# A hybrid decoder layer on one core: the exponential's bias on VectorE, and one more key block of every score tile turned by DMA

## The chip, the cores and the metric

The kernel runs on one core of a Trainium2 chip. The metric is the device time of one execution in microseconds (us). Of three runs the median is 2559.99 us, from 2559.71 to 2565.13. Engine names as in the profile: PE is TensorE's matrix multiplication and PEld its weight load, DVE is VectorE, ACT is ScalarE, POOL is GpSimd, SP is the engine whose queue issues most DMAs.

## The reference, cut to what matters

One decoder layer on a sequence of 2048 rows of 1024 columns. Eight attention heads of 64 columns stand beside a short gated convolution, and a convolved feed-forward network follows. The change lies in the attention:

```python
fcum = jnp.cumsum(logf, axis=1)
for i in range(s // BLOCK_Q):                 # blocks of 128 queries
    logits = jnp.einsum('bqhd,bkhd->bhqk', qb, kb) * scale
    logits = logits + fcum[:, :, q0:q1, None] - fcum[:, :, None, :q1]
    logits = jnp.where(causal[None, None], logits, -jnp.inf)
    p = jax.nn.softmax(logits, axis=-1).astype(v.dtype)
    outs.append(jnp.einsum('bhqk,bkhd->bqhd', p, vb))
```

Each block of 128 queries needs the keys up to its own end, so block i has i + 1 key blocks of 128.

## The kernel before, in words

Values are kept as two halves, a rounded high part and the rest, and a product is three products of halves. The layer runs in stages: modulation, norm and value projection; keys and queries; the gated convolution; attention (631 to 975 us of the profile); output projection, and the feed-forward network.

**Units.** The attention works in units. A unit is one head and two query blocks, 15 - u and u, so that every unit has 16 - u and u + 1, together NT + 1 = 17 key blocks. There are 8 units a head and 64 in all. The unit's scores stand in one tile `s_t` of 128 queries x 2176 keys.

**Steps.** The loop at line 798 runs one step a unit. In step s it interleaves four generators, one piece of each in turn, in this order: `turn` of unit s - 2, `scores` of unit s, `weights` of unit s - 1, `values` of unit s - 4. `K` (line 136) keeps these instructions in program order on each engine, so each engine's order is the order in which the pieces are emitted:

- `scores` (line 690): TensorE multiplies queries and keys in chunks of up to 512 keys; for each of the unit's five chunks one VectorE instruction (line 706) adds the key's forget term and keeps the row's maximum in `mx`, which a short second instruction of the same line reads out. `un["mx"]` is a view of two columns of `mx`, the last maximum of each of the two query blocks.
- `weights` (line 716): ScalarE makes the bias `nb` = `mx` x `qk[5]` + LN_PS (line 720, 128 x 2), then two exponentials in place (line 723), one for each query block, with `nb` as their bias and a row sum as second output.
- `turn` (line 727): the weights are turned, keys to partitions. The first WB = 10 key blocks are turned by TensorE (line 743) into two buffers of PSUM, in groups of 4, 4 and 2 blocks; ScalarE copies each group to 16 bits (line 745), and VectorE makes the rest (line 750), both into `near`. The other NT + 1 - WB = 7 blocks are split by two GpSimd instructions (lines 734 and 735) into the tile `wide`, and a transposing DMA on SP's queue (line 736) writes them to `far`.
- `values` (line 764): TensorE multiplies the turned weights and the values, a block of `near` or `far` at a time; ScalarE scales the result by the reciprocal of the row sum (line 781), which VectorE makes at the end of `turn` (line 762).

**Around it.** Seven times, while a head's units run, the next head's keys and queries are loaded step by step (`load_head`, line 580); the last two of its steps are GpSimd copies of keys (line 594). After the last head `mixed` (line 881) begins the output projection: weights of `w_out` are loaded (line 908) and multiplied by the gates on GpSimd (line 909), activations are loaded (line 911), and both are split in halves (lines 866 and 867).

**Scales.** `gain_scales` (line 422) fills the six columns of `qk`, a tile of its own (line 106): scales of queries and keys, their product in column 3, its reciprocal in column 4, and minus that in column 5. The tile `cst` (line 97) holds 128 columns of transposed parameters, of which columns 0 to 89 are written.

Of the kernel before, what the change touches and what calls it, by code (L numbers as in the profile page):

```python
# [8 lines left out]
F32 = mybir.dt.float32  # L9
# [4 lines left out]
AF = mybir.ActivationFunctionType  # L14
ALU = mybir.AluOpType
# [4 lines left out]
P = 128  # L20
# [11 lines left out]
NEG = -1.0e38  # L32
LN_PS = 9.704060527839234
WU = (NT + 1) * P
WB = 10
LEAD = 1
GROUP = 2
MID = 7
# [6 lines left out]
def kernel(  # L45
# [20 lines left out]
    V, A, G, T = nc.vector, nc.scalar, nc.gpsimd, nc.tensor  # L66
# [4 lines left out]
    const = ctx.enter_context(tc.tile_pool(name="const", bufs=1))  # L71
# [25 lines left out]
    cst = const.tile([P, P], F32, name="cst")  # L97
# [5 lines left out]
    sh2 = const.tile([P, KD], F32, name="sh2")  # L103
    cact = const.tile([P, KD], F32, name="cact")
    gq = const.tile([P, 2], F32, name="gq")
    qk = const.tile([P, 6], F32, name="qk")
    gates = const.tile([P, 2 * D], F32, name="gates")
    halo = const.tile([P, 2 * NPAIR, 2], F32, name="halo")
    G.memset(halo, 0.0)
# [26 lines left out]
    K = tc.keep_in_program_order  # L136
# [508 lines left out]
    with ExitStack() as ph:  # L645
        cs = ph.enter_context(tc.tile_pool(name="cs", bufs=6))
# [26 lines left out]
        def product(g):  # L673

            if len(products) > g:
                return
            while len(products) < min(g + GROUP, len(chunks)):
                h, u, _, i, c0, cw, last = chunks[len(products)]
                kh, qs, kl, nf = heads[h]
                qt = qs[:, i * P : (i + 1) * P]  # L680
                ps = ps_s.tile([P, 512], F32, tag="s", name="ps")
                K(T.matmul(ps[:, 0:cw], lhsT=qt, rhs=kh[:, c0 : c0 + cw], start=True, stop=False))  # L682
                K(T.matmul(ps[:, 0:cw], lhsT=qt, rhs=kl[:, c0 : c0 + cw], start=False, stop=not last))  # L683
                if last:
                    K(T.matmul(ps[:, cw - P : cw], lhsT=ident_b, rhs=maskb, start=False, stop=True))
                products.append(ps)
# [3 lines left out]
        def scores(un):  # L690

            nf = heads[un["h"]][3]
            un["s"] = s_t = cs.tile([P, WU], F32, tag="s", name="s_t", bufs=3)
            mx = cs.tile([P, 4, 4], F32, tag="mx", name="mx")[:, 0:2, :]
            un["l"] = cs.tile([P, 2], F32, tag="l", name="l", bufs=12)
            un["parts"] = [(NT - 1 - un["u"], NT - un["u"], 0), (un["u"], un["u"] + 1, NT - un["u"])]
            ends = [0, 0]
            while taken[0] < len(chunks) and chunks[taken[0]][:2] == (un["h"], un["u"]):
                _, _, p, i, c0, cw, last = chunks[taken[0]]
                o0 = p * (NT - un["u"]) * P  # L700
                product(taken[0] + LEAD)
                ps = products[taken[0]]
                products[taken[0]] = None
                taken[0] += 1
                g = c0 // 512
                K(V.tensor_tensor_reduce(  # L706
                    out=s_t[:, o0 + c0 : o0 + c0 + cw], in0=ps[:, 0:cw], in1=nf[:, c0 : c0 + cw], scale=1.0,
                    scalar=-3.0e38 if g == 0 else mx[:, p, g - 1 : g],
                    op0=ALU.add, op1=ALU.max, accum_out=mx[:, p, g : g + 1],
                ))  # L710
                if last:
                    ends[p] = 4 * p + g
                yield
            un["mx"] = mx.rearrange("p a g -> p (a g)")[:, ends[0] : ends[1] + 1 : ends[1] - ends[0]]

        def weights(un):

            s_t = un["s"]
            nb = cs.tile([P, 2], F32, tag="nb", name="nb")
            K(A.activation(nb, un["mx"], AF.Copy, scale=qk[:, 5:6], bias=LN_PS))  # L720
            for p, (_, n, b0) in enumerate(un["parts"]):
                cols = s_t[:, b0 * P : (b0 + n) * P]
                K(A.activation(cols, cols, AF.Exp, bias=nb[:, p : p + 1], scale=qk[:, 4:5], accum_out=un["l"][:, p : p + 1]))  # L723
                yield
            un["wide"] = wide = cp.tile([P, 2, WU - WB * P], F16, tag="wide", name="wide", bufs=3)

        def turn(un):

            s_t = un["s"]
            near = cp.tile([P, 2, WB, P], F16, tag="near", name="near", bufs=3)  # L730
            far = cp.tile([P, 2, NT + 1 - WB, P], F16, tag="far", name="far", bufs=3)
            un["t"] = near, far
            wide = un["wide"]
            K(G.tensor_scalar(wide[:, 0, :], s_t[:, WB * P : WU], 1.0, 0.0, op0=ALU.mult, op1=ALU.add))
            K(G.tensor_tensor(wide[:, 1, :], s_t[:, WB * P : WU], wide[:, 0, :], op=ALU.subtract))  # L735
            nc.sync.dma_start_transpose(far.rearrange("p a b n -> p (a b) n"), wide.rearrange("p a n -> p (a n)"))
            late = []

            def blocks(b0):
                nb = min(4, WB - b0)  # L740
                pt = ps_x.tile([P, 512], F32, tag="x", name="pt")
                for b in range(nb):
                    K(T.transpose(pt[:, b * P : (b + 1) * P], s_t[:, (b0 + b) * P : (b0 + b + 1) * P], ident))  # L743
                th, tl = [near[:, a, b0 : b0 + nb, :].rearrange("p b n -> p (b n)") for a in range(2)]
                K(A.activation(th, pt[:, 0 : nb * P], AF.Copy))  # L745
                late.append((tl, pt[:, 0 : nb * P], th))
# [51 lines left out]
        for s in range(H * nu + 8):  # L798
            h, u = divmod(s, nu)
            run = []  # L800
            if h < H:
                if u == 0:
                    steps = []
                    if h + 1 < H:
                        heads[h + 1], steps = load_head(h + 1)
                    if h % 2 == 0:
                        if h:
                            v16.append(load_values(h // 2))
                        at = cp.tile([P, NT, P], F32, tag="at", name="at")
                elif h + 1 < H:  # L810
                    steps[u - 1]()
                units.append({"h": h, "u": u, "at": at})
            for back, stage in ((2, turn), (0, scores), (1, weights), (4, values)):
                if 0 <= s - back < H * nu:
                    run.append(stage(units[s - back]))
            if s >= 16 and s % 16 in (0, 4):
                slow.append(store(units[s - 5]["at"], (s - 16) // 16, (0, 3) if s % 16 == 0 else (1, 2)))
            if s == H * nu:
                st.close()
                fq = end.enter_context(tc.tile_pool(name="fq", bufs=2, side="right"))  # L820
                ps_d = end.enter_context(tc.tile_pool(name="ps_d", bufs=4, space=PSUM, side="right"))
            n = 0
            while run or n < 3:
                run = [g for g in run if next(g, 1) is None]
                n += 1
                if n == 3:
                    slow = [g for g in slow if next(g, 1) is None]
# [388 lines left out]
```

## Time and profile before

| | |
|---|---|
| median of three runs | 2559.99 us |
| time of the profiled execution | 2562.44 us |
| its span, first to last instruction | 2560.5 us |
| mean granted TensorE clock | 0.992 |
| busy over the span: PE, DVE, ACT, POOL | 96%, 71%, 46%, 14% |
| nb on ScalarE (line 720), 64 times | 0.297 us each |
| wide on GpSimd (lines 734 and 735), 64 times each | 0.938 and 1.894 us each |

A row of the timeline gives start and duration in us, engine, line, operation, what it writes and reads, partitions x elements, and in brackets the idle time of the engine ahead of it with what ended it. A row of a group gives the count behind x, then busy us, mean ns of one, and idle time before. The stage of the change has an ACT share far above the 46% of the whole span, so its rows are read from windows of that stage.

### The profile page before, as it was taken

The numbers are of one execution on the slowest core, as the hardware profiler recorded it, in microseconds if no ns is written. First come the engines' busy times: TensorE is split into PE (matmuls) and PEld (weight loads), VectorE is DVE, ScalarE is ACT, GpSimd is POOL, SyncE is SP. The second block draws the span as 40 slices with busy tenths as digits, with TensorE's granted clock in tenths as the row PEclk, the third lists the DMA queues.
The fourth block names the chain that finished last, engine by engine and source line by source line (L and its number), as shares of the span: only waits on it lengthen the run. The fifth ranks groups of instructions, "written<-read, shape, count | busy, mean of one in ns | idle before, by whom it ended". The sixth has DMA issues, their size and how long they took to land.

```text
span 2560.5 us, 38478 instructions
## 1 busy us (share of the span) xinstructions
PE 2458.1 (96%) x14493; PEld 1995.7 (78%) x14493; DVE 1820.9 (71%) x3294; ACT 1183.2 (46%) x1932; POOL 357.8 (14%) x314
## 2 busy tenths in 40 slices
PE   4999999999999998998999999999999999999999
PEld 4988788887677776877888888877778888888887
DVE  7567874433888886676888888667768888885554
ACT  3522231111899994654444444455434444444333
POOL 4211010112656554110000000000000000000000
PEclk9999999999999999999999999999999999999999
DMA  8332563314697757332222222676632222226775
GB/s 237 140 104 59 153 177 103 99 54 122 122 187 154 162 96 236 116 111 94 83 83 74 83 83 83 210 233 209 218 125 75 86 80 81 81 84 191 226 234 188
DMA packets 400291, 341.43 MB, mean 133 GB/s; under 512 B 166545, under 2 KB 310249, under 8 KB 399081
## 3 DMA queue, kind: packets, MB, share of 16 engines
q1 hardware_dynamic: 392920, 322.13, 44.2%
q10 hardware_dynamic: 4752, 8.46, 0.9%
q0 software_dynamic: 2432, 8.39, 0.9%
q8 instruction: 113, 1.85, 0.3%
q14 instruction: 74, 0.60, 0.1%
HBM read 244.47 MB, written 65.08 MB: 121 GB/s over the span
## 4 chain that ended last, share of the span: by engine, by line
PE 50%; DVE 2%; DMA 1%; ACT 1%; issue 0%; SPq 0%; DVEq 0%; ACTq 0%
PE acc L1068 34%; PE acc L140 16%; DMA t<-x_sc 1%; DVE lo L867 1%; PE pt L956 0%; DVE t L949 0%; DVE t L876 0%; DVE t L875 0%; ACT junk L979 0%; ACT hi L866 0%; DVE b22l L867 0%; DVE lo L1023 0%; DVE t L966 0%; ACT t L958 0%; DVE w L986 0%
## 5 line engine op out<-in xcount | busy, mean ns | idle before, releaser
L140 PE MATMUL acc<-hi 128*128 128x512 f32 x960 | 378.2, 394 | 13.5 <-ACT hi L866 11.7
L140 PE MATMUL acc<-hi,lo 128*128 128x512 f32 x960 | 376.6, 392 | 0.8 <-DVE lo L867 0.7
L140 PE MATMUL acc<-lo,hi 128*128 128x512 f32 x960 | 375.9, 392 | 0.3 <-DVE lo L867 0.3
L867 DVE TENSOR_TENSOR lo<-raw,hi 128x1024 fp32r<-128x1024 f32 (+1 forms) x208 | 236.2, 1142 | 182.3 <-ACT hi L866 181.8
L866 ACT ACTIVATE hi<-raw 128x1024 fp32r<-128x1024 f32 (+1 forms) x208 | 205.0, 991 | 247.6 <-PE acc L140 207.6
L1081 DVE SCALAR_TENSOR_TENSOR w<-w,fcw,w 128x1024 f32<-128x1024 f32 x176 | 225.9, 1284 | 42.4 <-ACT w L1076 39.1
L1020 ACT ACTIVATE hi<-raw 128x1024 fp32r<-128x1024 f32 x132 | 139.4, 1057 | 221.4 <-PE acc L1068 212.7
L140 PEld LDWEIGHTS acc<-hi 128*128 128x128 f32 x960 | 181.3, 189 | 53.0 <-ACT hi L866 12.5
L140 PEld LDWEIGHTS acc<-hi,lo 128*128 128x128 f32 x960 | 181.2, 189 | 40.8 <-DVE lo L867 2.7
L140 PEld LDWEIGHTS acc<-lo,hi 128*128 128x128 f32 x960 | 181.2, 189 | 37.7 <-DVE lo L867 1.2
L1023 DVE TENSOR_TENSOR lo<-raw,hi 128x1024 fp32r<-128x1024 f32 x132 | 161.0, 1221 | 10.7 <-ACT hi L1020 10.6
L723 ACT ACTIVATE s_t<-s_t,nb,qk 128x2048 f32<-128x2048 f32 (+15 forms) x128 | 164.7, 1288 | 5.8
L140 PE MATMUL pr<-hh,wh 128*128 128x512 f32 x384 | 153.6, 400 | 0.0
L140 PE MATMUL pr<-hl,wh 128*128 128x512 f32 x384 | 151.5, 394 | 0.0
L140 PE MATMUL pr<-hh,wl 128*128 128x512 f32 x384 | 151.2, 394 | 0.0
L750 DVE TENSOR_TENSOR near<-pt,near 128x512 f16<-128x512 f32 (+1 forms) x192 | 114.9, 599 | 47.0 <-ACT near L745 47.0
L743 PE MATMUL pt<-ident,s_t 128*128 128x128 f32 x640 | 102.1, 284 | 26.2 <-DVE near L750 24.2
L706 DVE CUSTOM_DVE_ANT_0 s_t<-ps,nf,mx 128x512 f32<-128x512 f32 (+1 forms) x192 | 123.3, 642 | 2.7
L735 POOL TENSOR_TENSOR wide<-s_t,wide 128x896 f16<-128x896 f32 x64 | 121.2, 1894 | 5.4
L682 PE MATMUL ps<-kh,qs 128*128 128x512 f16 (+1 forms) x320 | 109.9, 347 | 2.0 <-ACT bt L635 1.1
L683 PE MATMUL ps<-kl,qs 128*128 128x512 f16 (+1 forms) x320 | 109.6, 347 | 0.0
L140 PE MATMUL acc<-wh,hh 128*128 128x512 f32 x256 | 103.6, 405 | 0.0
(303 smaller groups left out, 6226.0 us busy)
## 6 DMA issues: line engine op xcount, KB each, us to landing
raw<-in_w_up_dram SPq DMA_DIRECT2D x88, 512.0 KB, 3.7
raw<-y_sc SPq DMA_DIRECT2D x176, 256.0 KB, 3.9
raw<-in_w_down_dram SPq DMA_DIRECT2D x176, 256.0 KB, 4.2
y_sc<-w SPq DMA_DIRECT2D x44, 512.0 KB, 2.6
wm<-in_w_ada_dram SPq DMA_DIRECT2D x128, 128.0 KB, 2.6
wr<-in_w_in_dram SPq DMA_DIRECT2D x40, 256.0 KB, 4.3
x_t<-in_x_dram SPq DMA_DIRECT2D x16, 512.0 KB, 5.4
wa<-in_w_ada_dram SPq DMA_DIRECT2D x16, 512.0 KB, 6.4
```

The lines of the kernel that those rows point to most:

```text
L140: ins = T.matmul(acc, lhsT=a, rhs=b, start=st, stop=sp)
L682: K(T.matmul(ps[:, 0:cw], lhsT=qt, rhs=kh[:, c0 : c0 + cw], start=True, stop=False))
L706: K(V.tensor_tensor_reduce(out=s_t[:, o0 + c0 : o0 + c0 + cw], in0=ps[:, 0:cw], in1=nf[:, c0 : c0 + cw], scale=1.0, scalar=-3.0e38 if g == ...
L723: K(A.activation(cols, cols, AF.Exp, bias=nb[:, p : p + 1], scale=qk[:, 4:5], accum_out=un["l"][:, p : p + 1]))
L735: K(G.tensor_tensor(wide[:, 1, :], s_t[:, WB * P : WU], wide[:, 0, :], op=ALU.subtract))
L750: K(V.tensor_tensor(tl, pt, th, op=ALU.subtract))
L866: A.activation(hi, raw, AF.Copy, scale=HS)
L867: V.tensor_tensor(lo, raw, hi.bitcast(F32), op=ALU.subtract)
L1020: K(A.activation(hi, raw, AF.Copy, scale=HS))
L1023: K(V.tensor_tensor(lo, raw, hi.bitcast(F32), op=ALU.subtract))
L1068: K(T.matmul(acc, lhsT=a, rhs=b, start=st, stop=sp, skip_group_check=True))
L1081: K(V.scalar_tensor_tensor(y, u[:, m : m + 1024], fcw[:, m * 44 + ct : m * 44 + ct + 1], y, op0=ALU.mult, op1=ALU.add))
```

## The change

Three edits. The scales `qk` become six unused columns of `cst`. WB goes from 10 to 9: the third group that TensorE turns has one block in place of two, and `wide` and `far` hold 8 blocks in place of 7. And `nb` is made in `scores`, by VectorE, directly behind the maximum that completes the pair, in place of ScalarE ahead of the exponentials. Lines behind 713 stand two lines lower in the changed kernel.

```diff
-WB = 10
+WB = 9
...
-    qk = const.tile([P, 6], F32, name="qk")
+    qk = cst[:, 96:102]
...
                 if last:
                     ends[p] = 4 * p + g
+                if last and all(ends):
+                    m2 = mx.rearrange("p a g -> p (a g)")[:, ends[0] : ends[1] + 1 : ends[1] - ends[0]]
+                    un["nb"] = nb = cs.tile([P, 2], F32, tag="nb", name="nb")
+                    K(V.tensor_scalar(nb, m2, qk[:, 5:6], LN_PS, op0=ALU.mult, op1=ALU.add))
                 yield
-            un["mx"] = mx.rearrange("p a g -> p (a g)")[:, ends[0] : ends[1] + 1 : ends[1] - ends[0]]
 
         def weights(un):
 
             s_t = un["s"]
-            nb = cs.tile([P, 2], F32, tag="nb", name="nb")
-            K(A.activation(nb, un["mx"], AF.Copy, scale=qk[:, 5:6], bias=LN_PS))
+            nb = un["nb"]
```

On VectorE, in the middle of the stage, from the rest of a unit's third near group to the first chunk of the next unit (L706 with `s_t` is a chunk of scores, L706 with `mx` alone reads the maximum), before:

```order
L750 TENSOR_TENSOR near<-pt,near 128x256
L706 ISA s_t,mx<-ps,nf,mx 128x512
L706 ISA mx 128x1
L762 RECIPROCAL l<-l 128x2
L706 ISA s_t,mx<-ps,nf,mx 128x128
L706 ISA mx 128x1
L706 ISA s_t,mx<-ps,nf 128x512
```

and after:

```order
L752 TENSOR_TENSOR near<-pt,near 128x128
L706 ISA s_t,mx<-ps,nf,mx 128x512
L706 ISA mx 128x1
L764 RECIPROCAL l<-l 128x2
L706 ISA s_t,mx<-ps,nf,mx 128x128
L706 ISA mx 128x1
L716 TENSOR_SCALAR nb<-mx,cst 128x2
L706 ISA s_t,mx<-ps,nf 128x512
```

The near rest is half as wide, and the bias stands between the unit's last maximum and the next unit's first chunk.

On SP's queue, at the end of the attention (L792, later L794, stores an attention result; L908, later L910, loads a weight of the output projection, and L911, later L913, an activation), before:

```order
L736 DMA_TRANSPOSE far<-wide 128x14x128
L792 DMA m_at_74<-tm 128x512
L908 DMA wo<-in_w_out_dram 128x512
L792 DMA m_at_74<-tm 128x512 x2
L911 DMA src<-m_cv_75 128x512
L908 DMA wo<-in_w_out_dram 128x512
```

and after:

```order
L738 DMA_TRANSPOSE far<-wide 128x16x128
L794 DMA m_at_74<-tm 128x512 x3
L910 DMA wo<-in_w_out_dram 128x512
L913 DMA src<-m_cv_75 128x512
L910 DMA wo<-in_w_out_dram 128x512
```

The transposing DMA has 16 pieces in place of 14, and the first weight is issued behind the last two stores.

## The prediction

> **What bounds the kernel now.** The change touches one stage, the attention, so I read first the table of busy time by window for its steady part (columns: window, its length, then busy time and count of PE, PEld, DVE, ACT, POOL, then granted PE clock, DMA share, GB/s).
>
> ```profile
> 660.00:960.00 300.00, 279.77 (x4193) 216.29 (x4191) 258.83 (x793) 271.56 (x578) 182.97 (x125) 1.00 0.74 147
> ```
>
> No engine is full: TensorE has 93%, ScalarE 91%, VectorE 86%, GpSimd 61%, at a full clock. So the stage runs at the pace of a loop through several engines, and the timeline shows which. ScalarE (start, duration, what) from one unit's exponentials to the next:
>
> ```profile
> 756.50 0.30 ACT L720 ACTIVATE nb<-mx,qk 128x2 f32<-128x2 f32 x1
> 756.89 2.10 ACT L723 ACTIVATE s_t<-s_t,nb,qk 128x2048 f32<-128x2048 f32 x1
> ...
> 758.99 0.48 ACT L723 ACTIVATE s_t<-s_t,nb,qk 128x128 f32<-128x128 f32 x1
> ...
> 759.47 0.36 ACT L745 ACTIVATE near<-pt 128x256 f16<-128x256 f32 x1
> ...
> 760.29 1.34 ACT L745 ACTIVATE near<-pt 128x512 f16<-128x512 f32 x2
> 761.75 0.30 ACT L720 ACTIVATE nb<-mx,qk 128x2 f32<-128x2 f32 x1
> 762.14 1.99 ACT L723 ACTIVATE s_t<-s_t,nb,qk 128x1920 f32<-128x1920 f32 x1
> ```
>
> VectorE in the same unit, from its wait for ScalarE's third near block to the last maximum:
>
> ```profile
> 759.86 0.42 DVE L750 TENSOR_TENSOR near<-pt,near 128x256 f16<-128x256 f32 x1 [0.56 <-ACT near L745]
> ...
> 760.87 0.16 DVE L762 RECIPROCAL l<-l 128x2 f32<-128x2 f32 x1
> 761.09 0.62 DVE L706 CUSTOM_DVE_ANT_0 s_t<-ps,nf,mx 128x384 f32<-128x384 f32 x1
> 761.64 0.08 DVE L706 DVE_READ_ACCUMULATOR2_ANT mx<- 128x1 f32 x1
> 761.64 0.69 DVE L706 CUSTOM_DVE_ANT_0 s_t<-ps,nf 128x512 f32<-128x512 f32 x1
> ```
>
> The loop of this unit is: two exponentials, 756.89 to 759.47 = 2.58 us; third near block on ScalarE, its rest on VectorE, the last two score chunks, the maximum ready at 761.64 + 0.08 = 761.72, 2.25 us after the exponentials' end; 0.03 us to nb; nb to the next exponential 0.39 us. Together 5.25 us, the distance of the two wide exponentials. GpSimd works beside it:
>
> ```profile
> 759.64 0.94 POOL L734 TENSOR_SCALAR wide<-s_t 128x896 f16<-128x896 f32 x1 [2.46 <-ACT s_t L723]
> 760.66 1.90 POOL L735 TENSOR_TENSOR wide<-s_t,wide 128x896 f16<-128x896 f32 x1
> ```
>
> It starts 0.17 us after the second exponential ends and is done at 762.56, 3.09 us after it. Nobody in the loop waits for it today. Over the whole stage, the first exponential of the first unit and that of the 64th:
>
> ```profile
> 631.17 2.09 ACT L723 ACTIVATE s_t<-s_t,nb,qk 128x2048 f32<-128x2048 f32 x1
> 963.52 1.35 ACT L723 ACTIVATE s_t<-s_t,nb,qk 128x1152 f32<-128x1152 f32 x1
> ```
>
> That is 332.35 us for 63 steps, 5.275 us each.
>
> **Part 1, the bias on VectorE.** ScalarE loses nb, 0.39 us of the loop. VectorE gets a TENSOR_SCALAR from SBUF to SBUF, two columns, behind the maximum at 761.64 and ahead of the next unit's first chunk. How long does such an instruction take beside GpSimd? The trace has no two-column TENSOR_SCALAR there, so I look at the nearest rows: L514 (8 columns), L450 (1 column) and the two-column reciprocal. First the spreads (min/median/max in ns), then the rows with GpSimd's beside them.
>
> ```profile
> L514 DVE TENSOR_SCALAR r<-r x32: 152/400/550, 164.5 to 355.1; 128x8 f32<-128x8 f32 x32
> ```
>
> ```profile
> L762 DVE RECIPROCAL l<-l x64: 153/160/165, 639.4 to 970.3; 128x2 f32<-128x2 f32 x64
> ```
>
> ```profile
> 217.18 0.62 POOL L134 TENSOR_SCALAR th<-tf 128x512 f16<-128x512 f32 x1 [5.37 <-ACT tf L494]
> ```
>
> ```profile
> 217.34 0.14 DVE L450 TENSOR_SCALAR vs<-vs 128x1 int32<-128x1 int32 x1
> 217.46 0.37 DVE L514 TENSOR_SCALAR r<-r 128x8 f32<-128x8 f32 x1
> ```
>
> ```profile
> 241.60 0.62 POOL L134 TENSOR_SCALAR th<-tf 128x512 f16<-128x512 f32 x1 [5.36 <-ACT tf L494]
> ```
>
> ```profile
> 241.70 0.55 DVE L514 TENSOR_SCALAR r<-r 128x8 f32<-128x8 f32 x1
> ```
>
> L514 takes 0.15 us alone, but where it begins inside a GpSimd instruction it ends 0.03 us after that instruction's end: 217.83 against 217.80, 242.25 against 242.22. It is held until GpSimd is done. The one-column form ran through untouched at 217.34, and so did the reciprocal at 760.87, inside GpSimd's 760.66 to 762.56. So the price of nb lies between 0.16 us (as the reciprocal) and "until GpSimd ends". I take the second: it is the same operation, type and memory as L514, with more than one column, and the unheld rows are another operation or a single column.
>
> [...]
>
> Does nb fall into a GpSimd instruction? From the third unit on the last maximum is ready inside one in all 62 units; the first and the last of them:
>
> ```profile
> 639.19 1.88 POOL L735 TENSOR_TENSOR wide<-s_t,wide 128x896 f16<-128x896 f32 x1
> ```
>
> ```profile
> 640.02 0.08 DVE L706 DVE_READ_ACCUMULATOR2_ANT mx<- 128x1 f32 x1
> ```
>
> ```profile
> 962.28 1.89 POOL L735 TENSOR_TENSOR wide<-s_t,wide 128x896 f16<-128x896 f32 x1
> ```
>
> ```profile
> 962.81 0.08 DVE L706 DVE_READ_ACCUMULATOR2_ANT mx<- 128x1 f32 x1
> ```
>
> The ready times are inside L735 (640.10 in 639.19 to 641.07, 962.89 in 962.28 to 964.17), as in the unit above (761.72 in 760.66 to 762.56). Behind a held nb stand, on VectorE, the next unit's first chunk and its near rests; ScalarE's exponential waits for nb itself. And GpSimd's next pair waits for that exponential. So a new loop closes: exponentials, GpSimd pair, nb, exponentials.
>
> **Part 2, 8 blocks by DMA.** GpSimd's pair goes from 896 to 1024 columns. Slopes from shorter instructions of the same engine, and a third row for later:
>
> ```profile
> L134 POOL TENSOR_SCALAR th<-tf 128x512 f16<-128x512 f32 x32 | 19.8, 620 | 170.7 <-ACT tf L494 170.7
> ...
> L594 POOL TENSOR_SCALAR kh<-kh 64x2048 f16<-64x2048 f16 x8 | 15.1, 1892 | 7.6 <-DMA kh<-k_hi 7.0
> ...
> L275 POOL TENSOR_TENSOR hl<-hf,hh 128x512 fp32r<-128x512 f32 x8 | 10.4, 1294 | 0.7
> ```
>
> The first: (940 - 620)/384 = 0.83 ns a column, +0.11 us. The second: (1900 - 1294)/384 = 1.58 ns, +0.20 us, or in proportion to the columns +0.27; I take +0.23, so 2.13 us. The pair then ends 3.09 + 0.11 + 0.23 = 3.43 us after the exponentials. TensorE loses one transpose a unit, ScalarE and VectorE half of the third near block (VectorE 0.69 us for 512 columns, 0.42 for 256: 0.13 less; ScalarE about as much). In the new loop none of this is late: it only lets nb wait longer. The transposing DMA grows by 2/14 of its 4.1 us to landing, and is read two units later:
>
> ```profile
> far<-wide SPq DMA_TRANSPOSE x64, 4.1
> ```
>
> It costs nothing in the loop, and 0 to 0.6 us (I take 0.3) once, behind the last unit, where GpSimd's 0.34 us is exposed too.
>
> **Part 3, the scales in cst.** Nothing: no later writer of that tile stands in the stage. Its instructions have the same shapes.
>
> **Part 4, the first load of w_out** is moved on SP's queue behind two stores:
>
> ```profile
> 971.92 0.43 SPq L908 DMA_DIRECT2D wo<-in_w_out_dram  x1
> ...
> 978.93 0.32 SPq L911 DMA_DIRECT2D src<-m_cv  x1
> 979.30 0.43 SPq L908 DMA_DIRECT2D wo<-in_w_out_dram  x1
> ```
>
> ```profile
> 976.04 1.26 POOL L909 TENSOR_TENSOR wo<-wo,gates 128x512 f32<-128x512 f32 x1 [6.85 <-DMA wo<-in_w_out_dram]
> 983.25 2.89 POOL L909 TENSOR_TENSOR wo<-wo,gates 128x512 f32<-128x512 f32 x2 [5.95 <-DMA wo<-in_w_out_dram]
> ```
>
> ```profile
> 977.99 0.69 DVE L867 TENSOR_TENSOR lo<-wo,hi 128x512 fp32r<-128x512 f32 x1 [7.57 <-ACT hi L866]
> 983.07 0.69 DVE L867 TENSOR_TENSOR lo<-src,hi 128x512 fp32r<-128x512 f32 x1 [4.39 <-ACT hi L866]
> ```
>
> Issued at 978.93 it would reach GpSimd 3.95 us later (as 979.30 to 983.25), end there at 984.14 and VectorE 0.69 us after that, 984.83 in place of src's 983.07: up to 1.8 us late, and 0 if the second weight, late anyway, sets the pace. I take 1.0.
>
> **The sum.** New loop: 2.58 (exponentials) + 3.43 (to the end of GpSimd's pair) + 0.03 (nb behind it) + 0.03 (to ScalarE, as maximum to nb today) = 6.07 us. VectorE's own column would be ready after 5.25 - 0.39 - 0.25 = 4.6 us, so nb stands held for some 1.4 us. 63 steps: 382.4 - 332.35 = +50.1 us. Ends: 6.03 (the second slope) gives +47.5; 6.24 (the second in proportion, and nb's full 0.16 behind the hold) gives +60.8. With the tail 0.34 + 0.3 + 1.0 = +1.6 (0.3 to 2.7): +51.7 us. The profiled execution has 2562.44 us, 2.45 above the median of 2559.99; forecast 2614.1 for it, 2611.7 on the median.
>
> **Rivals.**
> - **nb is not held** (it behaves as the reciprocal). Then the old loop loses 0.39 + 0.12 + 0.13 us and gains 0.16 + 0.03: 5.25 becomes 4.80, 63 x -0.45 = -28 us, with the tail 2533. For it: 64 two-column reciprocals at 153 to 165 ns. Against: L514. A hold of under 0.45 us a unit would still leave a gain; 0.84 us are left today of L735 behind the maximum (762.56 - 761.72), and 1.4 would be. Chance 0.14.
> - **Held only where the two maxima lie side by side** (units 0 to 3 of a head; in 4 to 7 they lie three columns apart): 31 x 0.80 - 32 x 0.45 = +10 us, 2572 with the tail. No row tells. Chance 0.05.
> - **GpSimd's 14 copies of the next heads' keys (1.89 us, L594) slip in ahead of the held nb**: 14 x 1.9 = +27 us more, 2638. For it: they are next on GpSimd's queue then; against: they have 2.8 us of idle time to run in behind nb. Chance 0.07.
> - **A hold so short that it eats the gain**, within 0.2% (about what a measurement of this kernel tells from no change): 0.04.
>
> **Numbers.** Held throughout: 0.70 without and 0.07 with late copies; its own range is 2605 to 2624 with the spread of the runs. The range of 2600 to 2638 holds both and some smaller hold, near 0.8. Slower 0.82, same 0.04, faster 0.14.
>
> **What would show it.** Right: the new TENSOR_SCALAR has a mean of 1.2 to 1.7 us and ends within 0.05 us of GpSimd's second instruction (2.1 to 2.17 us); wide exponentials stand 6.0 to 6.2 us apart; ScalarE idles over 1 us a unit ahead of them, released by VectorE's nb; VectorE no longer waits for near. Wrong: nb at 0.16 to 0.2 us and steps under 5 us, or steps of 6 us with a short nb, where something else would be late.

## The result, and the profile after

The changed kernel takes 2602.94 us (median of four runs, 2599.67 to 2604.86) beside 2561.37 us for the kernel before. The ratio is 1.0159, 95% interval 1.0141 to 1.0177: slower by 1.6%. The forecast was 2611.7 us, range 2600 to 2638. The profiled execution has 2601.74 us and a span of 2600.0 us, 39.6 us more than before.

**The pace of the stage.** The first and the 64th unit's first exponential, after:

```profile
628.79 2.10 ACT L725 ACTIVATE s_t<-s_t,nb,cst 128x2048 f32<-128x2048 f32 x1 [4.70 <-DVE nb L716]
```

```profile
1020.00 1.35 ACT L725 ACTIVATE s_t<-s_t,nb,cst 128x1152 f32<-128x1152 f32 x1 [1.60 <-DVE nb L716]
```

63 steps take 391.21 us, 6.21 each on average, where they took 332.35. Their median is 6.13 us. The same window of the steady part as before (columns as there):

```profile
660.00:960.00 300.00, 241.73 (x3481) 184.58 (x3480) 288.49 (x718) 218.10 (x441) 174.80 (x108) 0.97 0.67 144
```

TensorE fell from 93% to 81%, ScalarE from 91% to 73%. VectorE rose from 86% to 96%, but that isn't work, as the groups of the bias and of GpSimd's pair show (busy us and mean ns behind the bar):

```profile
L737 POOL TENSOR_TENSOR wide<-s_t,wide 128x1024 f16<-128x1024 f32 x64 | 136.4, 2131 | 5.3
L716 DVE TENSOR_SCALAR nb<-mx,cst 128x2 f32<-128x2 f32 x64 | 103.8, 1622 | 2.3
...
L736 POOL TENSOR_SCALAR wide<-s_t 128x1024 f16<-128x1024 f32 x64 | 67.0, 1047 | 169.2 <-ACT s_t L725 169.2
```

Two numbers a partition take 1.62 us. The timeline of one step shows why. VectorE, the last maximum of a unit, the bias, the next unit's first chunk:

```profile
799.15 0.08 DVE L706 DVE_READ_ACCUMULATOR2_ANT mx<- 128x1 f32 x1
799.26 1.81 DVE L716 TENSOR_SCALAR nb<-mx,cst 128x2 f32<-128x2 f32 x1
800.99 0.68 DVE L706 CUSTOM_DVE_ANT_0 s_t<-ps,nf 128x512 f32<-128x512 f32 x1
```

GpSimd in the same step and the next:

```profile
798.92 2.13 POOL L737 TENSOR_TENSOR wide<-s_t,wide 128x1024 f16<-128x1024 f32 x1
801.13 1.90 POOL L594 TENSOR_SCALAR kh<-kh 64x2048 f16<-64x2048 f16 x1
803.98 1.05 POOL L736 TENSOR_SCALAR wide<-s_t 128x1024 f16<-128x1024 f32 x1 [0.94 <-ACT s_t L725]
805.11 2.12 POOL L737 TENSOR_TENSOR wide<-s_t,wide 128x1024 f16<-128x1024 f32 x1
```

And ScalarE, from the near copies ahead of one wide exponential to the next wide one:

```profile
799.40 1.08 ACT L747 ACTIVATE near<-pt 128x512 f16<-128x512 f32 x2 [0.21 <-PE pt L745]
801.17 1.67 ACT L725 ACTIVATE s_t<-s_t,nb,cst 128x1536 f32<-128x1536 f32 x1 [0.68 <-DVE nb L716]
...
802.83 0.91 ACT L725 ACTIVATE s_t<-s_t,nb,cst 128x640 f32<-128x640 f32 x1
...
807.35 1.56 ACT L725 ACTIVATE s_t<-s_t,nb,cst 128x1408 f32<-128x1408 f32 x1 [1.44 <-DVE nb L716]
```

The maximum is there at 799.23, GpSimd's second instruction ends at 801.05, the bias at 801.07, and the exponential starts at 801.17. From the third unit on, all 62 biases end 0.02 to 0.03 us behind the end of an L737. The loop that the prediction drew is closed: exponentials, GpSimd's pair, bias, exponentials. The 6.18 us from 801.17 to 807.35 are this loop and nothing else. The copy of the next head's keys (801.13) runs behind the held bias, not ahead of it.

What is waited for (window 660 to 960; total us, times, longest):

```profile
PEld pt L745 <- DVE near L752: 62.0, 46, 2.2
...
ACT s_t L725 <- DVE nb L716: 39.3, 38, 1.7
ACT at L783 <- PE po L779: 26.3, 31, 2.5
ACT near L747 <- PE pt L745: 10.5, 44, 0.7
DVE near L752 <- ACT near L747: 7.4, 14, 0.9
```

ScalarE waits for the bias, and TensorE waits for the near rests that queue behind it on VectorE. The wait for the bias is some 0.8 us a unit (39.3 us in the 48 units of the window) and not over 1 us, as the prediction's sign had it, because ScalarE spends about as long ahead of it waiting for TensorE's results (lines 783 and 747, 26.3 and 10.5 us).

**The part that nobody expected.** From the output projection's first matmul to the end of the program the changed kernel is faster, by 19.9 us (the +39.6 us of the span are -2.4 ahead of the first exponential, +58.9 in the 63 steps, +3.0 to the projection, -19.9 behind it). Nothing was changed there. A stretch of 410 us of the feed-forward network's first half, all TensorE (line 1068, after 1070), before and after:

```profile
1890.00:2300.00 410.00, 410.00 (x1760) 329.60 (x1759) 336.76 (x375) 179.19 (x248) 0.00 (x0) 1.00 0.25 80
```

```profile
1960.00:2370.00 410.00, 410.00 (x1801) 337.68 (x1800) 345.14 (x380) 186.64 (x254) 0.00 (x0) 1.00 0.28 89
```

Same instructions, same clock, but 1801 matmuls in place of 1760: 410/1760 = 233.0 ns each before, 227.7 after. With 3696 such matmuls that is 3696 x 5.3 = 19.6 us, the whole of it.

### The profile page after: what moved, and what is told of

Read it like the earlier page. It is cut to its first block, busy times and chain, and to the rows that moved or that the text cites. A ratio compares the mean times of both kernels' runs of the same rounds, so it can differ in the third digit from the quotient of the medians.

```text
span 2600.0 us, 38442 instructions
## 1 busy us (share of the span) xinstructions
PE 2443.1 (94%) x14429; PEld 1998.9 (77%) x14429; DVE 1912.4 (74%) x3358; ACT 1167.0 (45%) x1868; POOL 380.9 (15%) x314
## 4 chain that ended last, share of the span: by engine, by line
PE 48%; DVE 2%; DMA 1%; ACT 0%; issue 0%; SPq 0%; ACTq 0%; DVEq 0%
PE acc L1070 32%; PE acc L140 16%; DVE lo L869 1%; DMA t<-x_sc 0%; DVE t L878 0%; PE pt L958 0%; DVE t L877 0%; DVE t L951 0%; DMA out_dram<-t 0%; DVE lo L1025 0%; DMA raw<-y_sc 0%; ACT hi L868 0%; DVE raw L1019 0%; DVE b22l L869 0%; ACT junk L981 0%
## 5 line engine op out<-in xcount | busy, mean ns | idle before, releaser
L725 ACT ACTIVATE s_t<-s_t,nb,cst 128x2048 f32<-128x2048 f32 (+15 forms) x128 | 164.6, 1287 | 58.9 <-DVE nb L716 58.5
L745 PE MATMUL pt<-ident,s_t 128*128 128x128 f32 x576 | 94.3, 290 | 78.9 <-DVE near L752 78.0
L737 POOL TENSOR_TENSOR wide<-s_t,wide 128x1024 f16<-128x1024 f32 x64 | 136.4, 2131 | 5.3
L745 PEld LDWEIGHTS pt<-ident,s_t 128*128 128x128 f32 x576 | 66.4, 145 | 90.0 <-DVE near L752 87.1
L706 DVE CUSTOM_DVE_ANT_0 s_t<-ps,nf,mx 128x512 f32<-128x512 f32 (+1 forms) x192 | 122.6, 638 | 2.6
L752 DVE TENSOR_TENSOR near<-pt,near 128x512 f16<-128x512 f32 (+1 forms) x192 | 105.3, 549 | 12.6 <-ACT near L747 11.6
```

The lines of the kernel that those rows point to most:

```text
L706: K(V.tensor_tensor_reduce(out=s_t[:, o0 + c0 : o0 + c0 + cw], in0=ps[:, 0:cw], in1=nf[:, c0 : c0 + cw], scale=1.0, scalar=-3.0e38 if g == ...
```

## The experiments

The theory after reading the result: the bias is held on VectorE while GpSimd runs (cause of the slow steps); and the scales' move shifted every tile behind them by 32 bytes, which made the second half's matmuls faster. By the built programs' addresses the moving operands of line 1068 start in each partition at 32 modulo 256 before, and at 0 modulo 256 after (176 of the 3696 start 64 bytes further on in each case); the other operand's tiles did not move. Every kernel below computes the whole layer. Each is given beside runs of the kernel before on the same chip (2560.2 to 2562.4 us).

**1. The bias alone.** The changed kernel with ten near blocks again and the scales in their own tile.

```diff
-WB = 9
+WB = 10
-    qk = cst[:, 96:102]
+    qk = const.tile([P, 6], F32, name="qk")
```

> Only the bias is moved to VectorE; 10 blocks are turned by TensorE and the scales keep their own tile. My theory (the bias is held until GpSimd's pair is done): the pair of 896 columns ends 3.09 us after the exponentials, so a step is 2.58 + 3.09 + 0.03 + 0.10 = 5.80 us, 63 x (5.80 - 5.275) = +33 us, with slow TensorE phases and the tail 2593 to 2600; the bias takes 1.2 to 1.6 us and ends 0.03 us after GpSimd's second instruction. Rival (the bias itself takes 1.8 us on VectorE, whatever GpSimd does): the same step of 6.1 to 6.2 us as in the changed kernel, 2615 and more.

Measured: 2593.67 us, ratio 1.0128 (1.0114 to 1.0142). Steps have a median of 5.78 us, matmuls of the first half 233.2 ns. The bias costs 32 us by itself; with the pair shorter by 0.34 us the loop is shorter by 0.35. In 62 units the bias takes 0.48 to 1.33 us, less than expected in many, but it ends 0.02 to 0.03 us behind GpSimd's second instruction in all of them: how long it takes follows from when it starts.

**2. The scales alone.** The kernel before with `qk = cst[:, 96:102]`.

> Only the scales are put into the constant tile. My theory (the 20 us that came back behind the attention come from the tiles behind the scales, which start 32 bytes lower, at multiples of 64): the matmuls of line 1068 go from 233.3 to 227 ns start to start, -20 us, 2540. Rival (they come from the attention's end or from the other two edits): within 3 us of before, matmuls at 233 ns.

Measured: 2539.23 us, ratio 0.9916 (0.9904 to 0.9929). Steps 5.275 us as before, matmuls 227.8 ns. Of the three edits the one that was costed at nothing is worth 22 us.

**3. The bias column by column.** The changed kernel, with each part's bias computed behind its own last maximum, so that no instruction has more than one column.

```diff
-                if last and all(ends):
-                    m2 = ...
-                    K(V.tensor_scalar(nb, m2, qk[:, 5:6], LN_PS, ...))
+                if last:
+                    K(V.tensor_scalar(nb[:, p : p + 1], mx[:, p, g : g + 1], qk[:, 5:6], LN_PS, ...))
```

> The changed kernel, with the bias made by two instructions of one column each, each right behind the last maximum of its query block. My theory (two columns take the hold, one column does not): each takes 0.14 to 0.17 us beside GpSimd, a step is 4.8 to 4.9 us, -25 us from before in the attention and -20 behind it, 2512 to 2520. Rival (the wait belongs to any VectorE instruction that reads a fresh maximum, or to the tile's dependency): each is held for 1 us or more, 2600 or slower.

Measured: 2534.38 us, ratio 0.9894 (0.9879 to 0.9909). The group of the bias, and what remains of ScalarE's wait (window 660 to 900):

```profile
L712 DVE TENSOR_SCALAR nb<-mx,cst 128x1 f32<-128x1 f32 x128 | 27.4, 214 | 4.6
```

```profile
ACT s_t L721 <- DVE nb L712: 4.5, 18, 0.4
```

One column is not held: 214 ns beside the same GpSimd pair. So the hold on the two-column form makes the steps slow; the gain was overestimated, since steps are 5.14 us and not 4.8 to 4.9. Two such instructions a unit cost VectorE's queue about 0.5 us, the wait behind the maximum's read-out included.

**4. The bias on ScalarE, the other two edits kept.**

Beside the kernel before:

```diff
-WB = 10
+WB = 9
-    qk = const.tile([P, 6], F32, name="qk")
+    qk = cst[:, 96:102]
```

> The changed kernel with the bias back on ScalarE: scales in the constant tile and 8 blocks by DMA alone. My theory: steps lose the 0.25 us of the narrower third near block, 5.0 to 5.15 us, -8 to -17 us in the attention, -20 behind it, 2524 to 2535. Rival (the eighth block by DMA is what slows the attention): steps of 6 us, 2590 or slower.

Measured: 2533.65 us, ratio 0.9892 (0.9878 to 0.9905), steps 5.108 us. So without the bias's move the change would have been a gain of 28 us.

**5. All but the scales' move.** The changed kernel with the scales in a tile of their own.

> The changed kernel with the scales in a tile of their own again, so that every tile behind them starts 32 bytes higher, as before. Theory (start addresses set the pace of the second half's matmuls): matmuls of line 1068/1070 at 233 ns again, 2622 to 2627 us, some 21 us above the changed kernel. Rival (the scales' place costs nothing, as the prediction said, and the 20 us have another origin, such as the bias or the third block group): 227 ns and 2600 to 2606 us.

Measured: 2624.93 us, ratio 1.0250 (1.0235 to 1.0266); matmuls 233.2 ns. Undone in the other direction, the edit is worth the same 22 us. This is also the kernel whose cost the prediction had summed: +62.6 us measured, +51.7 said.

**6. Eight blocks by DMA alone.** The kernel before with `WB = 9`.

> The kernel before with 8 of 17 key blocks turned by DMA, and nothing else. Theory (the old loop loses what the third near group gets shorter, GpSimd's longer pair stays hidden): steps of 5.10 to 5.15 us in place of 5.275, that is 8 to 11 us, less some 2 to 5 us of the ends: 2552 to 2558 us. By the prediction's own terms, 0.25 us a step less, it would be 2545 to 2548. Rival (GpSimd's longer pair becomes late): at or above 2561.

Measured: 2552.11 us, ratio 0.9965 (0.9953 to 0.9978), steps 5.107 us on average: 10.6 us less over 63 of them. Where the bias is made on ScalarE, GpSimd's longer pair stays hidden; but the gain is 0.17 us a step, not 0.25. Every second step falls by 0.24 us, the steps between them by 0.02 to 0.13.

**7. A pad of 32 bytes.** Is it the address, or that the scales lie in `cst`?

```diff
     qk = const.tile([P, 6], F32, name="qk")
+    const.tile([P, 8], F32, name="pad")
```

> The kernel before with one unused tile of 32 bytes put behind the scales, and nothing else: the scales stay a tile of their own, and everything behind starts 32 bytes further on, at a multiple of 64. Theory (the start address alone): matmuls of the second half at 227 ns, 2538 to 2543 us, as with the scales in the constant tile. Rival (what helped was that the scales lie in the constant tile): 233 ns and 2559 to 2564 us.

Measured: 2546.13 us, ratio 0.9949 (0.9935 to 0.9963), matmuls 229.2 ns. An unused tile makes the kernel 16 us faster, so it is the address. But 229.2 is neither of the two values expected: a multiple of 64 is not the whole rule.

**8 and 9. Pads of 96 and of 224 bytes**, `[P, 24]` and `[P, 56]` in place of `[P, 8]`.

> The kernel before with an unused tile of 96 bytes behind the scales: the second half's moving operands start at 0 modulo 128 (128 modulo 256), where before has 32, the 32-byte pad 64, and the scales in the constant tile 0 modulo 256. Matmuls took 233.2, 229.2 and 227.8 ns there. Theory (a start at a multiple of 128 is the fast one): 227.8 ns, 2537 to 2543 us. Rival (only multiples of 64 matter, and the 1.4 ns between the two have another origin; or the pace falls until 256): 229 ns, 2543 to 2549 us.

Measured: 2554.68 us, ratio 0.9973 (0.9964 to 0.9982), matmuls 232.2 ns. A miss for both theories: the start at 128 modulo 256 is slower than the one at 64 (229.2 ns in run 7).

> The kernel before with an unused tile of 224 bytes behind the scales: the second half's moving operands start at 256 modulo 512. So far the matmuls took, by the start modulo 512: 0, 227.8 ns; 32, 233.2; 64, 229.2; 128, 232.2. Theory (0 modulo 256 is the fast start): 227 to 228 ns, 2537 to 2544 us. Rival (the fast start is further apart, 0 modulo 512 or more, or it is the distance to the other operand): 229 to 234 ns, 2546 to 2564 us.

Measured: 2540.02 us, ratio 0.9921 (0.9908 to 0.9935), matmuls 227.8 ns. The same 410 us of the first half with the pads of 32, 96 and 224 bytes, one row each; the second count is that of the matmuls:

```profile
1890.00:2300.00 410.00, 410.00 (x1790) 335.95 (x1789) 342.84 (x379) 184.94 (x255) 0.00 (x0) 1.00 0.26 84
```

```profile
1890.00:2300.00 410.00, 410.00 (x1768) 332.95 (x1767) 339.28 (x376) 182.36 (x252) 0.00 (x0) 1.00 0.26 82
```

```profile
1890.00:2300.00 410.00, 410.00 (x1802) 337.72 (x1801) 346.90 (x382) 187.09 (x258) 0.00 (x0) 1.00 0.27 87
```

| start modulo 256 | kernel | matmul to matmul, mean | kernel time |
|---|---|---|---|
| 0 | scales in `cst` | 227.8 ns | 2539.2 us |
| 0 | pad 224 | 227.8 ns | 2540.0 us |
| 64 | pad 32 | 229.2 ns | 2546.1 us |
| 128 | pad 96 | 232.2 ns | 2554.7 us |
| 32 | before | 233.2 ns | 2561.4 us |

Two quite different places with the same start modulo 256 agree within 1 us. Why that start is the fast one stays open: the other operand's tiles start at multiples of 256 as well, so these runs can't tell the start itself from its distance to the other operand, and every other tile behind the scales moved along.

**10. Three columns.** Which two-column forms are held? First, does an odd number escape?

```diff
+                    w = 3 if un["u"] < 4 else 2
+                    m0, m1 = (2, 5) if w == 3 else (ends[0], ends[1] + 1)
...
+                    un["nb"] = nb3[:, w - 2 : w]
```

> The changed kernel with the bias of units 0 to 3 of each head computed over three columns side by side (the two wanted and a neighbour) in place of two; units 4 to 7 keep their two columns. Theory (any TENSOR_SCALAR of more than one column from SBUF to SBUF is held): both forms end 0.02 to 0.03 us behind GpSimd's second instruction, 2599 to 2606 us. [...]

Measured: 2602.97 us, ratio 1.0164 (1.0150 to 1.0178). A three-column bias, and the GpSimd instruction that it lies in:

```profile
789.02 1.54 DVE L719 TENSOR_SCALAR nb<-mx,cst 128x3 f32<-128x3 f32 x1
```

```profile
788.41 2.13 POOL L740 TENSOR_TENSOR wide<-s_t,wide 128x1024 f16<-128x1024 f32 x1
```

790.56 against 790.54: held, as the two-column form is in the other units. Three columns are no way out.

**11. Two sources.** The added constant comes from two columns in SBUF, filled once ahead.

```diff
+V.memset(cst[:, 104:106], LN_PS)
...
-K(V.tensor_scalar(nb, m2, qk[:, 5:6], LN_PS, op0=ALU.mult, op1=ALU.add))
+K(V.scalar_tensor_tensor(nb, m2, qk[:, 5:6], cst[:, 104:106], op0=ALU.mult, op1=ALU.add))
```

> The changed kernel with the bias made by one SCALAR_TENSOR_TENSOR over the two columns: the added constant comes from a second tile in SBUF in place of the instruction itself. [...]

Measured: 2602.20 us, ratio 1.0162 (1.0149 to 1.0176).

```profile
801.85 1.80 DVE L717 SCALAR_TENSOR_TENSOR nb<-mx,cst 128x2 f32<-128x2 f32 x1
```

```profile
801.50 2.14 POOL L738 TENSOR_TENSOR wide<-s_t,wide 128x1024 f16<-128x1024 f32 x1
```

803.65 against 803.64: held too. The form with two inputs in SBUF is no way out either.

**12. The same two columns, with an accumulator.**

```diff
-K(V.tensor_scalar(nb, m2, ..., op0=ALU.mult, op1=ALU.add))
+K(V.tensor_scalar(nb, m2, ..., op0=ALU.mult, op1=ALU.add, accum_out=mx[:, 1, 3:4]))
```

> The changed kernel with the same two-column TENSOR_SCALAR, which now also writes the sum of its columns to an unused column. [...] Theory B (every TENSOR_SCALAR of two columns is held): steps of 6.1 to 6.3 us, 2597 to 2615 us.

Measured: 2529.34 us, ratio 0.9877 (0.9864 to 0.9891), the fastest of all: 1.2% under the kernel before, 2.8% under the changed one, by an output that nobody reads. VectorE in one step, and GpSimd's second instruction beside it:

```profile
796.34 0.08 DVE L706 DVE_READ_ACCUMULATOR2_ANT mx<- 128x1 f32 x1
796.45 0.22 DVE L716 TENSOR_SCALAR_CACHE_REDUCE nb<-mx,cst 128x2 f32<-128x2 f32 x1
796.60 0.08 DVE L716 DVE_READ_ACCUMULATOR nb<-mx,cst 128x1 f32 x1
796.60 0.69 DVE L706 CUSTOM_DVE_ANT_0 s_t<-ps,nf 128x512 f32<-128x512 f32 x1
```

```profile
795.71 2.13 POOL L737 TENSOR_TENSOR wide<-s_t,wide 128x1024 f16<-128x1024 f32 x1
```

```profile
796.77 1.99 ACT L725 ACTIVATE s_t<-s_t,nb,cst 128x1920 f32<-128x1920 f32 x1
```

The bias begins 0.74 us into GpSimd's instruction, is done at 796.67, and the exponential starts at 796.77 while GpSimd goes on to 797.84. Steps are 5.06 us on average.

So the form with an accumulator ran free (0.22 us), where three columns (1.54 us), two sources (1.80 us) and the plain two-column form (1.62 us on average in the changed kernel) ended with GpSimd's instruction. What tells these forms apart in the hardware was not shown.

## Why the prediction was right, and where it was not

**Right: the step on which the sign rested.** Part 1 chose "until GpSimd ends" over 0.16 us from one analogous row, L514. The bias behaved as L514 does, in 62 units of 62, and runs 1, 3 and 12 show that nothing else makes the steps slow: the bias alone brings the slow steps, and the same change with a bias that isn't held is faster than before.

**Right: in the new loop the eighth block only lets the bias wait longer.** GpSimd's instructions took 1.047 and 2.131 us (1.05 and 2.13 said). The longer pair, hidden in the old loop (run 6), is paid in full in the new one: 5.78 us with 7 blocks, 6.13 with 8.

**Failed: Part 3, "The scales in cst. Nothing."** It looked for later writers and for the shapes of the instructions, and not at the tiles that lie behind `qk`. They moved by 32 bytes, and that gave 22 us back (runs 2 and 5). So that the forecast came within 9 us is partly luck, two errors that offset each other: without that edit the kernel has 2624.93 us, 13.2 above the forecast.

**Mis-sized: the step of 6.07 us.** Most steps have 6.12 to 6.20. The bias does end 0.02 us behind GpSimd, but from there to the exponential it is 0.10 us, not 0.03 (801.07 to 801.17). The first two steps are shorter, so 57 steps have 6.105 us on average: 57 x 0.035 = +2.0 us. The other six have 6.88 to 7.57 us and are a mechanism that the prediction did not have. One of them, after; first its window, with the granted clock as the third number from the end:

```profile
698.00:705.00 7.00, 7.00 (x94) 5.25 (x91) 6.96 (x18) 4.56 (x10) 5.07 (x3) 0.76 0.55 104
```

```profile
700.17 1.81 DVE L716 TENSOR_SCALAR nb<-mx,cst 128x2 f32<-128x2 f32 x1
```

```profile
700.88 0.31 ACT L783 ACTIVATE at<-po,l 128x64 f32<-128x64 f32 x1 [1.55 <-PE po L779]
701.84 1.09 ACT L747 ACTIVATE near<-pt 128x512 f16<-128x512 f32 x2 [0.65 <-PE pt L745]
702.83 1.66 ACT L725 ACTIVATE s_t<-s_t,nb,cst 128x1536 f32<-128x1536 f32 x1
```

Here the bias is ready at 701.98, but the exponential starts at 702.83. TensorE ran at half its clock for 3.41 us, its values and transposes came late, and ScalarE had waited for them, 1.55 and 0.65 us, in instructions that the program order of `K` puts ahead of the exponential. Seven such windows of 3.41 us lie between the first and the last unit's first exponential after (an eighth follows at 1022.71), none before. Each of the six long steps holds one of them; the seventh lies in a step of 6.15. The six long steps add 6.8 us, together with the 2.0 the 8.8 us by which the 63 steps were longer than said.

**The rest of the sum.** The output projection's first matmul, before and after:

```profile
983.09 0.80 PE L140 MATMUL acc<-hi 128*128 128x512 f32 x1 [7.84 <-ACT hi L866]
```

```profile
1042.55 0.79 PE L140 MATMUL acc<-hi 128*128 128x512 f32 x1 [9.08 <-ACT hi L868]
```

From the last unit's first exponential that is 19.6 us (963.52 to 983.09) and 22.6 us (1020.00 to 1042.55): +3.0 for the tail, +1.6 said. The tail belongs to the eighth block: it has 19.6 to 20.0 us in the six kernels with ten near blocks and 22.4 to 22.8 in the eight with nine, wherever the bias is made; how it divides between the terms of Part 2 and of Part 4 wasn't tested. First exponential: 2.4 us earlier, not foreseen; over all the traces it lies between 628.7 and 631.6 us and follows no edit. From the projection on: -19.9. Together, against the 2614.1 us said for the profiled execution: +8.8 + 1.4 - 2.4 - 19.9 = -12.1, which gives 2602.0 beside the measured 2601.74.

**Mis-read: the old loop, and with it the price of "not held".** That rival did not happen, and its price was wrong as well: steps of 4.80 us, 28 us less. Run 12 is that case and has 5.06. Of the terms, the eighth block gives 0.17 us a step, not 0.25 (run 6), and moving nb gives 0.05 (5.108 to 5.061, runs 4 and 12), not 0.20. The step that failed is the loop through the maximum: it was read in one unit and priced for all. In the kernel before, nb starts 0.03 us behind the read-out of the last maximum in 10 of the 64 units, the one that the prediction shows among them; in the other 54 the maximum had been ready for 0.07 to 1.40 us. The very next unit, before: ScalarE, and VectorE's last read-out:

```profile
765.88 0.31 ACT L781 ACTIVATE at<-po,l 128x64 f32<-128x64 f32 x1 [0.60 <-PE po L777]
766.35 1.08 ACT L745 ACTIVATE near<-pt 128x512 f16<-128x512 f32 x2 [0.16 <-PE pt L743]
767.32 0.30 ACT L720 ACTIVATE nb<-mx,qk 128x2 f32<-128x2 f32 x1
```

```profile
766.75 0.08 DVE L706 DVE_READ_ACCUMULATOR2_ANT mx<- 128x1 f32 x1
```

The maximum is there at 766.83, and nb waits until ScalarE is through with its near copies, which themselves stood behind waits for TensorE. A shorter way through VectorE to the maximum gains nothing in such a unit. In run 12 the exponential starts 0.10 us behind the bias in 30 units; in the other 34 the bias had been ready for 0.38 to 1.50 us. And part of ScalarE's work that went became waiting for TensorE's value products, run 4 and then run 12 (window 660 to 900):

```profile
ACT at L781 <- PE po L777: 8.6, 21, 0.6
```

```profile
ACT at L783 <- PE po L779: 15.4, 23, 0.9
```

The forecast itself took from the old loop no more than the exponentials' 2.58 us and the 0.03 us from maximum to nb, so this bore on the rivals' prices alone.

**The other rivals.** "Held only side by side" is refuted by the changed kernel itself: the 62 held biases are of all eight places in a head. "Copies slip in ahead" did not happen: the copy at 801.13 starts 0.06 us behind the bias, and the other 13 stand likewise.

## What to carry to other kernels

A tiny VectorE instruction beside a busy GpSimd was priced here by its form and not by its size (two columns 1.62 us on average, with an accumulator 0.22 us): look in the trace for an instruction of the same form that starts inside a GpSimd instruction, and see whether both end together; if so, try one column a time (214 ns each in run 3) or a form with an accumulator, both of which ran free here. When an edit removes or adds a tile, compare the start addresses of everything behind it before calling the edit free, and check a stage that was not edited for a changed pace (here 32 bytes, 233.2 to 227.8 ns a matmul and 22 us). Here a loop closed through two engines that had slack before was paid at the full length of both (a median step of 6.13 us), so the gain of a shifted instruction must be weighed against what it newly waits for. And a loop that is read in one step has to be found in the others before a gain is priced by it: here it set the pace in at most 10 of 64.

## What the runs showed of the hardware

- **Start address and matmul pace.** A 128x512 matmul of the feed-forward network's first half took 227.8 ns with its moving operand at 0 modulo 256 bytes, 229.2 at 64, 232.2 at 128 and 233.2 at 32. No cause was tested.
- **Half clock and TensorE's pauses.** In the changed kernel seven windows of 3.41 us at half clock came with TensorE 81% busy; its matmuls paused for over 1 us thirty times in the stage's 64 units, for 2.10 us at the longest. With the bias alone (run 1) there were 24 such pauses, 1.60 us at the longest, and one window; in the kernel before one, of 1.1 us, and no window. The other kernels with a held bias (runs 5, 10 and 11) have 29 to 32 such pauses and seven or eight windows, and runs 3, 4, 6 and 12 neither. That the windows follow from the pauses is read from these counts and was not tested.
- **A hold ends sharply.** 62 biases ended 0.02 to 0.03 us behind GpSimd's instruction, whatever had been left of it (they took 1.28 to 1.90 us).
